# A two-layer attention and retention model on one core: the retention layer's token tiles placed ahead of the preceding output phase, and each next head's first value products placed at the end of the head before

## The chip, the cores and the metric

The kernel runs on one core of one Trainium2 chip. The metric is the device time of one execution in microseconds (us). The time before is 1820.17 us, the median of three runs (1818.12 to 1822.04). The core's engines are PE (TensorE: matmuls, with PEld for its weight loads), DVE (VectorE), ACT (ScalarE), POOL (GpSimd) and SP (SyncE, which here issues the loads).

## What is computed

Two layers over 512 latent tokens and 256 context tokens of width 1024, in float32. Layer 0 is windowed attention and an FFN, layer 1 bidirectional retention and an FFN. Each part is a normed input with a modulation, a mixer or FFN, and a gated addition to the stream. The part that matters here is the retention of layer 1, cut to its core:

```python
q_x, k_x, v_x, g_x = split(h_x @ w_qkvg)        # 4 heads: q, k 256 wide; v, g 512 wide
k_c, v_c = split(h_c @ w_qkvg[:, qk:2*qk + v])  # keys and values of the context
q_x = rope_2d(q_x, tables); k_x = rope_2d(k_x, tables) * k_scale
# per head, forward and backward scans, each from its final context state:
#   out = (q k^T * decay) v + q state * decay
mu, var = mean(o), variance(o)                  # over the 512 values of a head
y = (o - mu) * rsqrt(var + EPS) * gn_gain
out_x = (silu(g) * y) @ w_o
x = x + mx[2] * out_x
x = x + mx[5] * swiglu(modulate(rms_norm(x), mx[3], mx[4]), w_in, w_out)
```

## The kernel before

**Products in three matmuls.** Every float32 operand is split into two parts, hi (a copy on ACT, L164 or L139) and lo (a subtraction on DVE, L165 or L140), and a product is three matmuls: hi·hi, lo·hi, hi·lo. Weights come from HBM in pieces of 128x1024 float32 (512 KB) through SP's queue into one of two raw buffers (`wraw`) and are split into tiles `whi` and `wlo`, of which four pairs go round: two in the resident pool `rp` and two in the stage's own pool (`w_parts`).

**Seven products.** The FFNs of both layers and the retention's projections save an eighth of the matmuls: 2x2 blocks are multiplied by a scheme with seven products instead of eight, for which sums of token tiles (`token_sums`, L1120) and sums of weight pieces (L1268 to L1272, L1300 to L1306, L1362) are made on DVE first. "11", "12" and "22" name plain blocks, and the numbers 1 to 4 sums. `product_v` (L1171) makes value and gate products, two tiles of 128 tokens with 512 columns, 12 matmuls each; `product_q` (L1160) makes keys and queries.

**The stages around the change.** The last FFN output of layer 0 is `output(prev, True)` (L1075): for all latent and then all context tiles, matmuls (L147 to L149), a gated addition on DVE (L252), squares for the next norm on ACT (L208), their sum on DVE or POOL (L209), and the latent statistics once the latent tiles are through (L197 ends them). Then the pools of layer 0's FFN close, and those of the retention open: `hR` on the right side of the memory (token tiles `aq`, `hc`, sums `sA`), `qw`, `qa`, `qp` on the left. `latent_norm` (L1141) makes the token tiles: L1144 norms a tile into `qk`, L1147 (ACT) and L1148 (DVE) make hi and lo. `strips` (L1196) makes a head's decay factors. `context_norm` (L1153) does the context's norm.

**One head** (loop at L1223, four times): first value products "11" and "12" and the context's (`cv`), keys, then the query and key sum products (L1275 to L1289), rotation of queries and keys (`rope_pair`, L1183, DVE, POOL, ACT, DVE in a row), gate and value products (L1309 to L1317), scores and accumulation over six key tiles (L1322 to L1356), two more gate products (L1366, L1369), the norm of the output (L1380 to L1391), the gating (L1396), 16 transposes on PE (L1402), their copies (L1407, L1408) into eight `qk` tiles, and the output (`out_tile`, L1413), eight tiles of 12 matmuls. In the last head the output runs by halves of the tokens (L1440), with the statistics and the norm of the last FFN in it, and its first weights (`first_weights`, L1432). `first_two` (L1520) then makes the first two gate and up projections of that FFN; inside its first one `second_half` asks for the statistics of the second half of the tokens.

**What sets the order.** The kernel is written against tile pools. A planner orders each engine's instructions at build time: of those that its own model of the run holds to be ready, the one that was written first goes first. The order is then fixed, and each engine works it down. A tile that is laid over an older one waits for that one's last reader, tile by tile. A pool on the right side takes its room from the top down, and its tiles lie upward in the order in which their names are first asked for. `after(a, b)` puts an instruction behind others without a wait of its own. PSUM has eight banks: `pj` (2) and in the retention `X`, `Y`, `Z` (2 each).

The order of a head's end, which the change takes apart:

```python
        product_v(Zg, quarter_of(4), w22, False)     # L1369, last gate product
        ...                                          # norm of ov, gates: L1380 to L1396
        tps = [W4("Z"), W4("Z"), pj(), pj()]         # L1399
        for n in (2, 3, 0, 1):
            for e in range(4):
                nc.tensor.transpose(tps[e][:, n * P:(n + 1) * P], gate[n][:, e * P:(e + 1) * P], ident)
```

Of the kernel before, what the change touches and what calls it, by code (L numbers as in the profile page):

```python
# [16 lines left out]
KT = D // P  # L17
# [32 lines left out]
def dit_kernel(ctx, tc, xT, cT, crow, small, consts, masks, tabs0, tabs1, jtab, adaQ, adaN, adaT, wst, out):  # L50
# [104 lines left out]
    def project_pair(ws, hs, os, between=None):  # L155

        for k in range(KT):
            for w, o in zip(ws, os):
                ins = mm3(o, (w[0][:, k * P:(k + 1) * P], w[1][:, k * P:(k + 1) * P]), hs[k], k == 0, k == KT - 1)
            if k == 2 and between:  # L160
                between([ins])
# [687 lines left out]
    hq = F.enter_context(tc.tile_pool(name="hq", bufs=1, reuse_waits="tile", side="right"))  # L849
# [224 lines left out]
    assert not ada_q  # L1074
    output(prev, True)  # L1075
# [11 lines left out]
    H = ExitStack()  # L1087
    hpool[0] = H.enter_context(tc.tile_pool(name="hR", bufs=1, reuse_waits="tile", side="right"))
# [5 lines left out]
    h_sum = [(T(hpool[0], 512, "sA", 16, F32R), T(hpool[0], 512, "sA", 16, F32R)) for _ in range(KT)]  # L1094
# [14 lines left out]
    def t_qk(dt=F32R):  # L1109
        return T(qp, 512, "qk", 8, dt)  # L1110
# [9 lines left out]
    def token_sums(hm, part, sh2, sums):  # L1120

        q1, q2 = HALVES
        shift = mods[1, 0][:, part]
        nc.vector.tensor_tensor(sh2[:, 0:4], shift[:, 0:4], shift[:, 4:8], op=add)
        for k in range(4):
            t1, t2 = hm[k], hm[k + 4]
            nc.vector.scalar_tensor_tensor(t2[:, q2], t1[:, q2], sh2[:, k:k + 1], t2[:, q2], add, add)
# [25 lines left out]
    def context_norm(behind):  # L1153
        rms(1, bank=pj, behind=behind)
        h_ctx.extend(norm_mod(1, 1, 0, cres)[0])
# [15 lines left out]
    def product_v(os, a, w, first):  # L1171

        for t, o in enumerate(os):
            tok = slice(t * P, t * P + P)
            for k in range(4):
                whi, wlo = (p[:, k % 2 * 512:k % 2 * 512 + 512] for p in w[k // 2])
                xhi, xlo = (x[:, tok] for x in a(k))
                for i, (p, r) in enumerate(((xhi, whi), (xhi, wlo), (xlo, whi))):
                    ins = nc.tensor.matmul(o, p, r, start=first and k + i == 0, stop=k == 3 and i == 2,  # L1179
                                           skip_group_check=not first)  # L1180
        return ins
# [38 lines left out]

    hm = latent_norm()
    dx, dcx = strips(0)
    for hd in range(RH):  # L1223
# [4 lines left out]
        b11 = [split_chunk(chunk(bv + i)) for i in range(2)]  # L1228
        b21 = [split_chunk(chunk(bv + i)) for i in (2, 3)]
        Yv, Xv, cv = [W4("Z"), W4("Z")], [W4("X"), W4("X")], [pj(), pj()]  # L1230
        ins = product_v(Yv, quarter_of("11"), b11, True)
        if hd == 0:
            context_norm([ins])
        vt = [T(rp, 512, "res", 12) for _ in range(4)]
        for t in range(2):
            nc.scalar.copy(vt[t], Yv[t])
        product_v(Xv, quarter_of("12"), b21, True)
# [8 lines left out]
        if hd == 0:  # L1246
            token_sums(hm, 0, T(qp, 64, "sh2", 1), h_sum)
# [43 lines left out]
        kh = rope_pair(kt, cos1, sin1)  # L1291
# [58 lines left out]
        pend = None  # L1350
        for m in range(6):
            cur = scores(m)
            if pend is not None:
                accumulate(m - 1, *pend)
# [44 lines left out]
        tps = [W4("Z"), W4("Z"), pj(), pj()]  # L1399
# [4 lines left out]
        for e in range(4):  # L1404
# [4 lines left out]
            yt.append((hi, lo))  # L1409
        wpos[0] = chunk_base + 16 * hd + 12  # L1410
# [18 lines left out]
        hF = ctx.enter_context(tc.tile_pool(name="hF", bufs=1, reuse_waits="tile", side="right"))  # L1429
# [8 lines left out]
        hF_parts = lambda: (T(hF, 1024, "whi", 2, F32R), T(hF, 1024, "wlo", 2, F32R))  # L1438
        ln_exp_turn()
        for i, c in enumerate(HALVES):  # L1440
            for d in range(KT):
# [4 lines left out]
                if (i, d) in ((1, 3), (1, 5)):  # L1446
                    first_weights(hF_parts)
                if i == 1 and d == 1:
                    hm += [T(hF, 512, "hm", 8) for _ in range(KT)]
                    off_grid(hF, 48)  # L1450
                    hx += [(T(hF, 512, "hx", 16, F32R), T(hF, 512, "hx", 16, F32R)) for _ in range(KT)]
                    off_grid(hF, 16)
# [18 lines left out]
    ring += [rp, rp, hF, hF, fp, fp]  # L1471
# [34 lines left out]
    def seven():  # L1506
        g, u = w_raw(fp, 2), w_raw()
        b11 = w_parts(fp, 4)
        b22 = T(hF, 512, "hm", 8, F32R), T(hF, 512, "hm", 8, F32R)
# [209 lines left out]
```

## Time and profile before

| what | value |
|---|---|
| median of three runs | 1820.17 us (1818.12 to 1822.04) |
| profiled execution | 1813.7 us, span 1811.9 us, mean granted clock 0.99 |
| ACT, POOL busy | 836.5 us (46%), 161.6 us (9%) |
| last output phase of layer 0, PE | 871.65 to 906.5 us |
| retention, first product to last output matmul | 908.20 to about 1462 us |
| heads 1, 2, 3 begin on PE | 1058.12, 1192.14, 1324.86 us |
| granted clock at one half, in span time | 909.5 to 923.1, 977.7 to 984.5, 1032.3 to 1039.2, 1435.1 to 1438.5 us |

The span runs from the first to the last instruction of the profiled execution; the execution's own time is 1.8 us more. A row of the time views gives start, duration, engine, line, operation, output and inputs, shapes and count, and in brackets how long the engine had been idle and what ended that. A row of waits gives the instruction, what it waited for, total, times and longest. The granted clock is the share of full speed that the throttle gave PE.

### The profile page before, as it was taken

Reading aid. Unit: us, or ns where it says so; the run is one execution under the profiler, and the core shown is the slowest. Engines: PE = TensorE matmul, PEld = TensorE weight load, DVE = VectorE, ACT = ScalarE, POOL = GpSimd, SP = SyncE. Lnnn points to the kernel's source line nnn. Section 1 sums busy time; section 2 is a strip of 40 time slices with the busy share of each in tenths; the row PEclk is TensorE's granted clock in tenths of the full one; section 3 lists DMA queues with packets and bytes.
Section 4 is the critical chain, followed back from the end, with each engine's and each line's share of the span. In section 5 each row is a group of like instructions: output and inputs, shape, how many; then the busy total and the mean of one; then the engine's idle time right before and its main releaser. Section 6 shows DMA issues by size and latency. Waiting matters only on the chain.

```text
span 1811.9 us, 27643 instructions
## 1 busy us (share of the span) xinstructions
PE 1728.4 (95%) x10876; PEld 1531.3 (85%) x10876; DVE 1347.3 (74%) x2327; ACT 836.5 (46%) x1461; POOL 161.6 (9%) x291
## 2 busy tenths in 40 slices
PE   6999999999999999999979998999999999999999
PEld 4777776799999999999867787787787899999998
DVE  6697786786689877777698747847848898777774
ACT  5477676362424343333464524524524564445442
POOL 0035344000000000000001001001001010000000
PEclk9999999999999999999989999999999999999999
DMA  9510002542244444343233523524423333234232
GB/s 350 212 45 16 24 2 82 186 140 94 82 140 128 152 127 141 119 148 117 72 128 117 164 70 116 165 72 128 155 78 109 111 95 97 90 117 117 83 93 82
DMA packets 59891, 206.69 MB, mean 114 GB/s; under 512 B 6640, under 2 KB 7024, under 8 KB 59504
## 3 DMA queue, kind: packets, MB, share of 16 engines
q1 hardware_dynamic: 52848, 179.75, 30.8%
q0 software_dynamic: 6912, 25.17, 4.6%
q8 instruction: 85, 1.39, 0.3%
q14 instruction: 46, 0.38, 0.1%
HBM read 202.80 MB, written 2.10 MB: 113 GB/s over the span
## 4 chain that ended last, share of the span: by engine, by line
PE 71%; DVE 15%; DMA 5%; ACT 4%; issue 2%; POOL 2%; DVEq 0%; ACTq 0%; POOLq 0%; SPq 0%
PE Y L834 13%; PE Z L834 6%; PE pj L149 6%; PE pj L148 6%; PE pj L147 6%; PE Z L1179 4%; DMA wraw<-in_wst_dram 3%; DVE wlo L165 3%; PE X L834 3%; PE pT L706 2%; PE pO L718 2%; PE S L683 2%; PE pj L1179 2%; PE X L147 1%; PE Y L147 1%
## 5 line engine op out<-in xcount | busy, mean ns | idle before, releaser
L164 ACT CAST whi<-wraw 128x1024 fp32r<-128x1024 f32 x173 | 180.9, 1051 | 307.7 <-PE Z L149 73.1
L165 DVE TENSOR_TENSOR wlo<-wraw,whi 128x1024 fp32r<-128x1024 f32 x173 | 211.1, 1223 | 52.2 <-ACT whi L164 51.7
L834 PE MATMUL Y<-aq,whi 128*128 128x384 f32 x576 | 156.0, 335 | 0.5 <-ACT hn L973 0.5
L252 DVE SCALAR_TENSOR_TENSOR res<-pj,mod,res 128x512 f32<-128x512 f32 (+1 forms) x112 | 81.6, 729 | 64.7 <-PE pj L149 63.6
L139 ACT CAST whi<-wraw 128x1024 fp32r<-128x1024 f32 x84 | 87.9, 1048 | 85.1 <-PE Z L149 23.5
L140 DVE TENSOR_TENSOR wlo<-wraw,whi 128x1024 fp32r<-128x1024 f32 x84 | 102.9, 1226 | 28.1 <-ACT whi L139 27.3
L834 PEld LDWEIGHTS Y<-aq,whi 128*128 128x128 f32 x576 | 104.8, 188 | 1.2 <-ACT hn L973 0.8
L834 PE MATMUL Y<-aq,wlo 128*128 128x384 f32 x288 | 96.5, 335 | 1.6 <-DVE wlo L165 1.6
L101 ACT ACTIVATE pr<-pr,stat,qs 128x513 f32<-128x513 f32 (+2 forms) x96 | 74.3, 776 | 30.7 <-DVE stat L690 29.8
L1179 PE MATMUL Z<-whi,sA 128*128 128x512 f32 x256 | 81.9, 397 | 2.4 <-ACT gate L1311 2.2
L697 POOL TENSOR_SCALAR pr<-pr,stat 128x512 f32<-128x512 f32 (+2 forms) x96 | 67.1, 713 | 86.5 <-DVE stat L694 66.4
L270 DVE CUSTOM_DVE_ANT_0 y<-adaw,crow,small_sb 128x1024 bf16<-128x1024 f32 x48 | 61.4, 1280 | 13.8 <-DMA adaw<-in_adaT_dram 13.7
L147 PE MATMUL pj<-ax,whi 128*128 128x512 f32 x176 | 68.8, 391 | 1.1 <-DVE res L252 1.1
L1190 POOL TENSOR_TENSOR hn<-hn,sq 128x512 f32<-128x512 f32 x16 | 28.9, 1819 | 448.1 <-DVE sq L1189 432.0
L149 PE MATMUL pj<-ax,whi 128*128 128x512 f32 x176 | 68.6, 390 | 0.0
L148 PE MATMUL pj<-ax,wlo 128*128 128x512 f32 x176 | 68.5, 389 | 0.0
L706 PE MATMUL pT<-const_sb,pr 128*128 128x128 f32 x352 | 58.1, 284 | 9.9 <-POOL pr L697 7.6
L147 PE MATMUL pj<-act,whi 128*128 128x512 f32 x168 | 66.0, 393 | 0.0
L148 PE MATMUL pj<-act,wlo 128*128 128x512 f32 x168 | 65.9, 392 | 0.0
L149 PE MATMUL pj<-act,whi 128*128 128x512 f32 x168 | 65.5, 390 | 0.0
L706 PEld LDWEIGHTS pT<-const_sb,pr 128*128 128x128 f32 x352 | 38.8, 141 | 30.4 <-POOL pr L697 18.4
L684 DVE CUSTOM_DVE_ANT_0 pr<-S,mask,qs 128x256 f32<-128x256 f32 (+1 forms) x96 | 53.1, 567 | 14.3 <-PE S L683 7.9
(504 smaller groups left out, 5363.3 us busy)
## 6 DMA issues: line engine op xcount, KB each, us to landing
wraw<-in_wst_dram SPq DMA_DIRECT2D x238, 512.0 KB, 3.6
adaw<-in_adaT_dram POOLq DMA_DIRECT2D x32, 512.0 KB, 3.9
wx<-in_wst_dram SPq DMA_DIRECT2D x24, 512.0 KB, 4.5
adan<-in_adaQ_dram SPq DMA_DIRECT2D x16, 512.0 KB, 7.8
adan<-in_adaN_dram SPq DMA_DIRECT2D x16, 512.0 KB, 8.2
crow<-in_adaT_dram POOLq DMA_DIRECT2D x16, 512.0 KB, 4.2
res<-in_xT_dram SPq DMA_DIRECT2D x16, 256.0 KB, 5.4
adaw<-in_adaT_dram SPq DMA_DIRECT2D x8, 512.0 KB, 4.0
```

What stands on the lines that cost most here:

```text
L101: ins = nc.scalar.activation(*args, **kw)
L139: nc.scalar.copy(hi, raw)
L140: nc.vector.tensor_tensor(lo, raw, hi, op=sub)
L147: nc.tensor.matmul(o, whi, xhi, start=first, stop=False)
L148: nc.tensor.matmul(o, wlo, xhi, start=False, stop=False)
L149: return nc.tensor.matmul(o, whi, xlo, start=False, stop=last)
L164: nc.scalar.copy(hi, t)
L165: return nc.vector.tensor_tensor(lo, t, hi, op=sub)
L252: return nc.vector.scalar_tensor_tensor(res[d], o, mods[l, s][:, part, d:d + 1], res[d], mult, add)
L706: nc.tensor.transpose(tp[:, a * P:(a + 1) * P], self.pr[(0, 2, 1, 3)[a]][:, ki * P:(ki + 1) * P], ident)
L834: nc.tensor.matmul(o, p, r, start=first and k + i == 0, stop=k == 3 and i == 2, skip_group_check=not first)
L1179: ins = nc.tensor.matmul(o, p, r, start=first and k + i == 0, stop=k == 3 and i == 2, skip_group_check=not first)
```

## The change

No instruction is added or taken away; they are placed and ordered otherwise.

- **Token tiles ahead of the output.** The pool `hq` of layer 0's operand sums closes before `output(prev, True)`, and `hR` opens there; the sums `sA` get a pool of their own (`hS`) after it. The `qk` tiles (the normed tokens, later rotated queries and keys, at last the gated output) move from `qp` on the left into `hR`. The ring of weight tiles begins anew there.
- **Order in the first head.** The first value product stands right behind the latent norm; token sums are put behind the context norm; the first decay strips come behind the token sums.
- **Head ends.** The next head's first value product (`values_first`) stands between gates and transposes, its first context product (`context_values`) between transposes and output. The transposes write the `X` and `Y` banks, which held the head's outputs.
- **Inside a head.** Y2 is copied before Y; the keys' rotation stands behind the weights of gates and values; the last value product is cut in two, with the first scores between the halves.
- **Last FFN.** Its pool `hF` becomes three, `hM`, `hW`, `hX`, in this order from the top; the statistics of the second half are asked for after the sixth step of the first projection, not the third.

```diff
     assert not ada_q
+    Q.close()
+    H = ExitStack()
+    hpool[0] = H.enter_context(tc.tile_pool(name="hR", ..., side="right"))
+    wsel[0] = 0
     output(prev, True)
...
-    H = ExitStack()
-    hpool[0] = H.enter_context(tc.tile_pool(name="hR", ..., side="right"))
+    hS = H.enter_context(tc.tile_pool(name="hS", ..., side="right"))
...
     def t_qk(dt=F32R):
-        return T(qp, 512, "qk", 8, dt)
+        return T(hpool[0], 512, "qk", 8, dt)
...
-    def product_v(os, a, w, first):
-        for t, o in enumerate(os):
+    def product_v(os, a, w, first, tiles=(0, 1)):
+        for t in tiles:
+            o = os[t]
...
+    def values_first(hd):
+        w = [split_chunk(chunk(chunk_base + 16 * hd + 4 + i)) for i in range(2)]
+        Y = [W4("Z"), W4("Z")]
+        ins = product_v(Y, quarter_of("11"), w, True, (0,))
+        product_v(Y, quarter_of("11"), w, True, (1,))
+        return w, Y, ins
+
+    def context_values(w):
+        c = [pj(), pj()]
+        product_v(c, context_half(0), w, True)
+        return c
+
     hm = latent_norm()
-    dx, dcx = strips(0)
+    ahead_v = values_first(0)
     for hd in range(RH):
-        b11 = [split_chunk(chunk(bv + i)) for i in range(2)]
+        b11, Yv, ins = ahead_v
+        if hd == 0:
+            normed = context_norm([ins])
         b21 = [split_chunk(chunk(bv + i)) for i in (2, 3)]
-        Yv, Xv, cv = [W4("Z"), W4("Z")], [W4("X"), W4("X")], [pj(), pj()]
-        ins = product_v(Yv, quarter_of("11"), b11, True)
-        if hd == 0:
-            context_norm([ins])
...
-        product_v(cv, context_half(0), b11, True)
+        if hd == 0:
+            cv = context_values(b11)
         product_v(cv, context_half(1), b21, False)
...
         if hd == 0:
-            token_sums(hm, 0, T(qp, 64, "sh2", 1), h_sum)
+            token_sums(hm, 0, T(qp, 64, "sh2", 1), h_sum, [normed])
+            dx, dcx = strips(0)
...
         product_q(Y2, quarter_of(1), w1, True)
+        for e, o in halves(Y2):
+            nc.scalar.copy(qt[e][:, HALVES[1]], o)
         product_q(Y, quarter_of(3), w3, False)
         for e, o in halves(Y):
-            nc.scalar.copy(qt[e][:, HALVES[1]], o)
-        for e, o in halves(Y2):
             nc.vector.tensor_tensor(qt[e][:, HALVES[1]], qt[e][:, HALVES[1]], o, op=add)
...
         qh = rope_pair(qt, cos1, sin1)
-        kh = rope_pair(kt, cos1, sin1)
...
             w4.append(split_chunk(v21))
+        kh = rope_pair(kt, cos1, sin1)
...
-        product_v(Yv, quarter_of("22"), w4, False)
-        for t in range(2):
+        def last_values(t):
+            product_v(Yv, quarter_of("22"), w4, False, (t,))
             nc.scalar.copy(vt[2 + t], Yv[t])
+        last_values(0)
...
-        pend = None
-        for m in range(6):
+        pend = scores(0)
+        last_values(1)
+        for m in range(1, 6):
...
-        tps = [W4("Z"), W4("Z"), pj(), pj()]
+        if hd < RH - 1:
+            ahead_v = values_first(hd + 1)
+        tps = [W4("X"), W4("X"), W4("Y"), W4("Y")]
...
             yt.append((hi, lo))
+        if hd < RH - 1:
+            cv = context_values(ahead_v[0])
...
         H.close()
-        hF = ctx.enter_context(tc.tile_pool(name="hF", ..., side="right"))
+        hM, hW, hX = (ctx.enter_context(tc.tile_pool(name=n, ..., side="right"))
+                      for n in ("hM", "hW", "hX"))
...
-                project_pair(ahead[2 * f:2 * f + 2], half(i), (go[:, c], uo[:, c]), None if i + f else second_half)
+                project_pair(ahead[2 * f:2 * f + 2], half(i), (go[:, c], uo[:, c]), None if i + f else second_half, 5)
```

The tiles `hm` now come from `hM`, the weights `whi` and `wlo` of the last FFN from `hW`, and the normed tokens `hx` from `hX`.

More of the change, by code (lines that the diff above doesn't have):

```diff
@@ L159, in project_pair @@
                 ins = mm3(o, (w[0][:, k * P:(k + 1) * P], w[1][:, k * P:(k + 1) * P]), hs[k], k == 0, k == KT - 1)
-            if k == 2 and between:
+            if k == at and between:
                 between([ins])
@@ L1093, in dit_kernel @@
     W4 = lambda n: T(psR, 512, n, 2)
[L1094 removed]
+    h_sum = [(T(hS, 512, "sA", 16, F32R), T(hS, 512, "sA", 16, F32R)) for _ in range(KT)]
     h_first = [T(hpool[0], 512, "aq", 12, F32R) for _ in range(4)]
@@ L1118, in operands, with token_sums @@
         return of
-    def token_sums(hm, part, sh2, sums):
+    def token_sums(hm, part, sh2, sums, behind=()):
         q1, q2 = HALVES
@@ L1126, in token_sums @@
             t1, t2 = hm[k], hm[k + 4]
-            nc.vector.scalar_tensor_tensor(t2[:, q2], t1[:, q2], sh2[:, k:k + 1], t2[:, q2], add, add)
+            after(nc.vector.scalar_tensor_tensor(t2[:, q2], t1[:, q2], sh2[:, k:k + 1], t2[:, q2], add, add), behind)
             nc.vector.tensor_tensor(t1[:, q2], t1[:, q1], t1[:, q2], op=sub)
@@ L1154, in context_norm @@
         rms(1, bank=pj, behind=behind)
-        h_ctx.extend(norm_mod(1, 1, 0, cres)[0])
+        h, last = norm_mod(1, 1, 0, cres)
+        h_ctx.extend(h)
+        return last
     def context_half(i):
@@ L1437, in dit_kernel @@
         wx_parts = lambda: (T(qw, 1024, "wx", 4, F32R), T(qw, 1024, "wx", 4, F32R))
-        hF_parts = lambda: (T(hF, 1024, "whi", 2, F32R), T(hF, 1024, "wlo", 2, F32R))
+        hW_parts = lambda: (T(hW, 1024, "whi", 2, F32R), T(hW, 1024, "wlo", 2, F32R))
         ln_exp_turn()
```

28 lines of the change are left out of this document (15 added, 13 removed).

## The prediction

> **What bounds the kernel now.** I read the page first, then who waited for whom on PE from 906 to 1475 us (the retention layer and the entry to the last FFN), then the order of time of PE, DVE, ACT and SP around each long wait, then busy sums by stage.
>
> The page:
>
> ```profile
> span 1811.9 us, 27643 instructions
> PE 1728.4 (95%) x10876; PEld 1531.3 (85%) x10876; DVE 1347.3 (74%) x2327; ACT 836.5 (46%) x1461; POOL 161.6 (9%) x291
> PE 71%; DVE 15%; DMA 5%; ACT 4%; issue 2%; POOL 2%; DVEq 0%; ACTq 0%; POOLq 0%; SPq 0%
> ```
>
> PE is the bound: 71% of the chain that ended last, busy 95%. A change that adds and removes no instruction, as this one, can only win where PE stands still or runs at a lower granted clock. Waits of PE in the stretch that is touched (us in total, times, longest):
>
> ```profile
> PE Z L1179 <- DVE wlo L165: 16.2, 8, 10.2
> PE X L147 <- ACT qk L1407: 5.7, 4, 1.6
> PE pj L1333 <- DVE hn L1338: 4.1, 3, 1.4
> PE Z L1402 <- DVE gate L1396: 3.5, 4, 1.2
> PE Z L1179 <- ACT gate L1311: 2.2, 2, 1.9
> PE pj L1333 <- ACT qk L164: 2.1, 1, 2.1
> PE Y L1167 <- DVE gate L1283: 1.9, 3, 1.0
> ...
> PE pj L216 <- POOL y L209: 1.4, 1, 1.4
> ```
>
> Together 37 us, and every one is a wait that the change moves. The longest, 10.2, is the entry to the retention layer: the first value product waits for its weights' low half. In order of time DVE explains it (start, duration):
>
> ```profile
> 906.46 0.48 DVE L252 SCALAR_TENSOR_TENSOR res<-Z,mod,res 128x256 f32<-128x256 f32 x1 [0.95 <-PE Z L149]
> 906.86 1.41 DVE L1144 SCALAR_TENSOR_TENSOR qk<-res,acol,y 128x512 f32<-128x512 f32 x2
> ...
> 917.83 1.21 DVE L165 TENSOR_TENSOR wlo<-wraw,whi 128x1024 fp32r<-128x1024 f32 x1
> ...
> 919.36 1.21 DVE L165 TENSOR_TENSOR wlo<-wraw,whi 128x1024 fp32r<-128x1024 f32 x1
> ```
>
> The latent norm (L1144, L1148) begins only after the last context add, the splits of the value weights follow behind it, and PE stands from 908.9 to 919.1. The same view at the end of a head, on PE:
>
> ```profile
> 1031.81 0.44 PE L1402 MATMUL Z<-const_sb,gate 128*128 128x128 f32 x2 [1.19 <-DVE gate L1396]
> 1032.08 0.38 PE L1402 MATMUL pj<-const_sb,gate 128*128 128x128 f32 x2
> 1033.68 0.79 PE L147 MATMUL X<-qk,whi 128*128 128x512 f32 x1 [1.22 <-ACT qk L1407]
> ```
>
> Transposes wait for gates, the output for the transposes' copies. Busy sums by stretch (length; busy of PE, PEld, DVE, ACT, POOL; granted clock; DMA):
>
> ```profile
> 909.50:923.10 13.60, 4.01 (x10) 3.14 (x11) 13.60 (x25) 7.17 (x14) 0.00 (x0) 0.50 0.55 207
> 1032.30:1039.20 6.90, 5.68 (x15) 4.36 (x14) 5.09 (x6) 4.12 (x6) 0.00 (x0) 0.51 0.57 172
> 901.30:906.50 5.20, 5.12 (x41) 4.74 (x40) 1.98 (x6) 2.15 (x5) 2.56 (x4) 1.00 0.00 0
> ...
> 906.50:1017.50 111.00, 94.90 (x494) 80.74 (x495) 98.18 (x145) 59.96 (x99) 8.67 (x6) 0.91 0.40 127
> ```
>
> The granted clock halves around these waits, and a 512-column matmul then starts every 0.43 us, not 0.227. And DVE is busy 98.2 of 111 us in the first head: close behind PE.
>
> **The change, part by part.** A value product of two tiles is 24 matmuls, 5.45 us at 0.227.
>
> (a) Entry and first head, 906.5 to 1017.5. The token tiles now lie where the FFN's operand sums lay; their last reader, the last seven-product, ends at 871.7. So L1144 can start once the latent statistics are there (L197, done 901.4), five us earlier, in DVE's gaps: 5.20 less 1.98 busy, 3.2 us, some 2.7 of it usable, two to three of the four operand tiles needed first (1.07 each: 0.67 and 0.40 from start to start). With that pool moved, the value weights' split tiles also lie on room free since 871.7 or in the resident pool. Their data landed at 875.7 and 881.7, and DVE is busy only 11.7 of the 21.3 us before 901.3, so four low halves (1.22 each, 4.9 us) fit before the end of the output. Then PE has no reason to wait at 906.5: two value products and the context product, 96 matmuls, take 21.8 us instead of the 36.6 to 943.06. That is 14.8. Behind it the first head has waits of 1.9 and 2.1 and half clock from 977.7 to 984.5 (some 2.3 lost): at most 21 for PE. DVE gives less: 98.2 less 7.6 moved ahead leaves 90.6, so no more than 20.4; if it keeps all its 12.8 idle, only 7.6. The token sums (about 11 us) now queue behind the context norm (6.8), and the decay strips (1.65) behind them; all have to be through when PE comes to the first sum product at about 940, and I add them up to about 943, a new wait of 3 us where there was none. I take the middle, **14 us**, ends 7.6 and 20.4.
>
> (b) Inside heads 1 to 3. Copying Y2 before Y takes L1283 off the path of the next product: 1.9 us. Half of the last value product now stands between the first and second scores: 12 matmuls, 2.7 us, over waits on L1338 of 1.35; I take 1.0 of each. Moving the key rotation behind the weight splits brings those splits 4 us of DVE work earlier; they cost waits of 0.37 and 1.36, 0.35 and 1.35, and 1.83; I take half, 2.6. Against it the keys come late: multiply, POOL (1.6 to 2.0), ACT, DVE in a row, two such, 6 us after its start; 0.5 a head. 1.9 + 3.0 + 2.6 - 1.5 = **6 us**, ends 2 and 10.
>
> (c) Three head ends. The next head's first value product (5.45) now fills the time between gates and transposes, its context product (5.45) that between transposes and output. From 1028.4 PE needs 5.45 + 1.8 (16 transposes) + 5.45 + 21.8 (output) + 10.9 (second value and context halves) = 45.4, to 1073.8, against 1079.88: 6.1, of which 2.8 is half clock. At the other two, 48.5 against 45.4: 3.1 each, 12.2 in all. What must be in time: two weight low halves on DVE by 1028.4 and 1029.8. The output's first two stood there, ending 1027.7 and 1029.4, with the same split tiles and the same two raw buffers; the value weights take these places, and the output's move some 4 us on, needed first at 1041. On SP the two value loads go ahead of four output loads (3.6 us to landing), with 12 us of PE work over them. The Z banks are free from 1026.5 and 1030, before each is needed. I take **11.5**, ends -6.3 and 12.2.
>
> [...] The row: half clock from 1032.3 to 1039.2, though the longest wait just before was 1.22 us. [...]
>
> (d) End of the last head. Nothing fills it, and the transposes now write the banks that hold the outputs, so none starts before the last gate product (1433.2); before, half of them were done by 1431.8. That puts some 12 transposes, 1.2 us, on the path, and the half-clock stretch (1435.1 to 1438.5, 1.4 us lost) may lengthen: **-2 us**, ends 0 and -3.
>
> (e) Entry to the last FFN. The statistics of the second half are now asked for three steps later (6 matmuls of 0.12 each), which takes away the 1.36 wait on POOL. But by the order of requests in the pools (16 KB each counted from the top) the tiles for weights three and four now lie on the 16 KB of the rotated tiles, which the output reads to its end at about 1462; two splits (ACT 1.05, DVE 1.22 each) that stood at 1445 to 1452 come in front of the norm's last tiles. PE has 5.8 us of the first gate and up before it needs them. **+0.7**, ends -3 and 1.4.
>
> **Sum.** 14 + 6 + 11.5 - 2 + 0.7 = 30.2 us off the profiled execution's 1813.7 (span 1811.9): 1783.5. The median of the runs, 1820.17, lies 6.5 above that execution; taken from the median, **1790.0**. With the ends that (a) to (e) reach without a new mechanism, 9.6 (taking 6 for c) and 44, it is 1776 to 1811.
>
> **Rivals.**
> 1. DVE becomes the bound but nothing gets worse. For it: 98.2 of 111 us, hardly a gap from 906 to 950. Then (a) 8, (b) 2, (c) 8.5, (d) -3, (e) -1: 14.5, 1805.7. Chance 0.22.
> 2. All covers hold: (a) 20, (b) 9, (c) 12.2, (d) and (e) -1: 40, 1780. Chance 0.08.
> 3. The clock isn't won back at the head ends: (c) is 8.7, 1792.8. A stretch with short waits and 128-column transposes can still be granted half. Chance 0.08. [...]
> 4. Slower: DVE works its queue in order, and what the change puts further back comes last while PE's matmuls stand behind it. Place and price: the context norm ends where it did (939.6), then token sums, strips, key weights' sums and one split, 19 us, to 959 against 954.6: -4.5, and no gain in the rest of the head; value weights behind the last gate product (1031.8), first usable 1032.9, PE idle 4.5 and then 1.7 lost at half clock: 0, -3.1, -3.1; keys late by 2 in each of three heads: -6; (d) -3, (e) -3. Together -22.7: 1842.9. It decides once the splits for the next head stand behind the last L1396 and the sums behind 940. Against it: DVE is half idle before 906, and the order of instructions is planned by when they are ready. Chance 0.07.
> 5. It doesn't do what it says: the norm still starts after the last context add, and head ends win as much as (d), (e) and late keys lose: within 3.6 us of 1820. Chance 0.05.
>
> **Numbers.** Forecast 0.50, at 1780 to 1800; rivals 0.22, 0.08, 0.08, 0.07, 0.05. Faster by over 0.2% (3.6 us, about what a measurement of this kernel can tell from no change): 0.50 + 0.22 + 0.08 + 0.08 = 0.88; same 0.05; slower 0.07. The range leaves out rivals 4 and 5: 1776 to 1811.
>
> **What would show it.** L1144 starting near 901 to 903 and the first L1179 near 906.5 with no wait of 10 us and full clock (a); a new PE wait at the first product with the token sums (a, rival 1); no wait on L1283, and shorter ones on L1338 and on the splits (b), or a new one on the keys (rival 4); value products between the last gate product and the transposes with no wait before them (c); later transposes in the last head (d); no wait on POOL L209, and how late the splits for weights three and four stand (e). The forecast is wrong if DVE's order puts the next head's splits behind the gates, or if a stall of more than some 6 us opens before the sum products.

## The result, and the profile after

The changed kernel takes 1812.9 us (median of 9 runs, 1811.3 to 1816.3) where the kernel before takes 1819.8 (9 runs beside them, 1816.2 to 1822.4): a ratio of 0.9963, 95% interval 0.9952 to 0.9974. It is faster by 6.9 us, where 30.2 were forecast, and lies above the range of 1776 to 1811.

The profiled execution took 1812.0 us, span 1810.2. Its page, the lines that answer to those of before:

```profile
span 1810.2 us, 27644 instructions
PE 1732.1 (96%) x10876; PEld 1538.7 (85%) x10876; DVE 1352.0 (75%) x2327; ACT 835.0 (46%) x1461; POOL 163.9 (9%) x291
PE 69%; DVE 16%; DMA 6%; ACT 4%; issue 3%; POOL 2%; SPq 0%; DVEq 0%; ACTq 0%; POOLq 0%
```

PE is still the bound, with the same instructions. The page can't tell where the time went; the stretches between the same matmuls of both traces can (start to start, us):

| stretch (part of the prediction) | before | after | gain | forecast |
|---|---|---|---|---|
| start to last output matmul ahead of the layer | 906.1 | 908.0 | -1.8 | 0 |
| (a) to the first key product | 36.9 | 32.4 | 4.6 | |
| (a) to the first sum product | 11.5 | 12.4 | -0.9 | |
| (a) to the first head's gate product behind the scores | 62.9 | 67.2 | -4.2 | |
| (a) together | 111.4 | 111.9 | **-0.5** | 14 |
| (b) heads 1 to 3, first sum product to gate product | 187.6 | 186.7 | **0.9** | 6 |
| (c) three head ends, gate product to next key product | 180.6 | 168.5 | **12.1** | 11.5 |
| (d) last head, gate product to the first statistics matmul | 33.0 | 34.3 | **-1.4** | -2 |
| (e) from there to the last FFN's first output product on Z | 58.2 | 66.0 | **-7.8** | 0.7 |
| to the last matmul | 296.4 | 296.2 | 0.1 | 0 |

The pair of profiles shows 1.7 us. The first row is code that the change leaves alone: over the profiled executions here the last output phase begins anywhere from 871.6 to 877.0 us, so one pair can be some 5 us off. The rows below it gain 3.5 in all; why the medians differ by 6.9, this one pair of profiles does not show.

The waits of PE in the stretch that was touched (us in total, times, longest) name what took the place of the old ones:

```profile
PE Z L1187 <- ACT gate L1336: 8.6, 3, 2.9
PE Z L1187 <- ACT whi L164: 5.3, 2, 3.6
PE Z L1187 <- DVE wlo L165: 4.6, 2, 4.0
PE Z L1187 <- ACT gate L1333: 2.7, 3, 0.9
PE X L147 <- ACT hx L241: 2.6, 2, 1.4
```

The 1.8 and 10.2 us at the entry are now 1.8, 1.1 and 4.0. New are three waits of 2.9, one in each later head, on ACT's copy of a gate product (L1336). Before, the same copy was waited for twice, by 0.5:

```profile
PE Z L1179 <- ACT gate L1314: 1.0, 2, 0.5
```

**The entry.** DVE and ACT of the changed kernel in order of time (start, duration):

```profile
899.48 1.23 DVE L165 TENSOR_TENSOR wlo<-wraw,whi 128x1024 fp32r<-128x1024 f32 x1 [0.59 <-ACT whi L164]
...
903.42 1.24 DVE L1149 SCALAR_TENSOR_TENSOR qk<-res,acol,y 128x512 f32<-128x512 f32 x1
...
904.97 0.74 DVE L1149 SCALAR_TENSOR_TENSOR qk<-res,acol,y 128x512 f32<-128x512 f32 x1
...
915.89 1.21 DVE L165 TENSOR_TENSOR wlo<-wraw,whi 128x1024 fp32r<-128x1024 f32 x1
917.03 0.74 DVE L1153 SCALAR_TENSOR_TENSOR aq<-qk,mod,aq 128x512 fp32r<-128x512 f32 x1
```

```profile
908.63 0.42 ACT L208 ACTIVATE sq<-res 128x256 f32<-128x256 f32 x1 [0.82 <-DVE res L252]
908.95 1.03 ACT L164 CAST whi<-wraw 128x1024 fp32r<-128x1024 f32 x1
```

The norm does start early, at 903.4. But of the first two value weights only one is split early, at 898.4 on ACT and 899.5 on DVE; its tile is in the resident pool. The other lies in the layer's own pool `qp`. By the layout of the pools its room had last been read at about 873, but the closed pool that held this room also held the activations that the output reads to its end. ACT splits it only at 908.95, 1.0 us behind the last output matmul, and its low half stands on DVE at 915.89 behind nearly the whole norm.

**The middle of the first head** (first sum product to gate product) was to lose its waits and its half clock; it became 4.2 us longer. Busy sums before and after (columns as in the prediction):

```profile
954.60:1017.50 62.90, 58.66 (x302) 49.57 (x301) 51.57 (x64) 31.05 (x49) 7.01 (x4) 0.95 0.43 132
```

```profile
952.70:1019.90 67.20, 60.92 (x301) 51.08 (x302) 56.35 (x69) 32.66 (x51) 6.94 (x4) 0.92 0.40 125
```

PE's waits there sum to 6.8 us (4.2 before), the longest 3.6 for a high half from ACT. The clock is at one half from 954.9 to 958.4 and from 975.4 to 982.2; before, only from 977.7 to 984.5. DVE is busy 4.8 us more in this stretch: work that stood ahead of the first sum product now stands behind it.

**Heads 1 to 3.** ACT and PE of the second head:

```profile
1116.79 0.62 ACT L164 CAST qk<-hn 128x512 fp32r<-128x512 f32 x1 [4.79 <-POOL hn L1198]
1117.32 0.58 ACT L1336 COPY gate<-Z 128x512 f32<-128x512 f32 x1
```

```profile
1114.68 0.39 PE L1187 MATMUL Z<-whi,sA 128*128 128x512 f32 x1
1117.95 0.50 PE L1187 MATMUL Z<-whi,aq 128*128 128x512 f32 x1 [2.88 <-ACT gate L1336]
```

```profile
1111.00:1117.90 6.90, 3.16 (x13) 2.17 (x12) 5.09 (x7) 2.10 (x4) 3.92 (x2) 1.00 0.60 205
1118.70:1122.10 3.40, 3.40 (x9) 2.60 (x9) 2.29 (x3) 1.47 (x2) 0.00 (x0) 0.51 0.24 45
```

The gate product is done at about 1115, but on ACT a copy of the rotated keys, which waits 4.8 us for POOL and starts at 1116.8, stands in front of the gate copy, which starts at 1117.3. PE's bank comes free 2.9 us late, and then the granted clock is 0.51 for 3.4 us (busy sums by stretch, as in the prediction).

**The entry to the last FFN.** DVE:

```profile
1446.82 0.42 DVE L197 SCALAR_TENSOR_TENSOR y<-sq,y 128x256 f32<-128x256 f32 x1
1447.41 0.48 DVE L1450 SCALAR_TENSOR_TENSOR res<-Y,mod,res 128x256 f32<-128x256 f32 x1 [0.16 <-PE Y L149]
...
1451.73 0.48 DVE L1450 SCALAR_TENSOR_TENSOR res<-X,mod,res 128x256 f32<-128x256 f32 x1 [0.96 <-PE X L149]
1452.13 1.74 DVE L238 SCALAR_TENSOR_TENSOR hm<-res,acol,y 128x256 f32<-128x256 f32 x3
```

The statistics are ready at 1447.2. DVE idles 0.96 us ahead of each of three output adds, and still the norm (L238) comes only at 1452.1, 4.9 us later, when PE is at the last output matmul (1452.9). It then goes ahead even of the last output add, which follows at 1458.8. Before, the norm came right behind the statistics, with output adds among its steps:

```profile
1456.26 0.48 DVE L197 SCALAR_TENSOR_TENSOR y<-sq,y 128x256 f32<-128x256 f32 x1
1456.77 1.36 DVE L238 SCALAR_TENSOR_TENSOR hm<-res,acol,y 128x256 f32<-128x256 f32 x2
1458.06 0.47 DVE L1421 SCALAR_TENSOR_TENSOR res<-X,mod,res 128x256 f32<-128x256 f32 x1
```

By the layout of the pools, the tiles that the norm writes lie on the context's normed tiles (`hc`), which the last head's context products read last: their room was free.

**Theory.** T1: the order of each engine is written when the program is built; there, an instruction on a tile of a pool that is opened over a closed one stands behind the last reader of that whole pool, though the tile's own room may have been read for the last time long before (here at about 873, by the layout of the pools). It holds the first value weight at the entry, and at the FFN the norm, whose room lay in one pool with the rotated tiles. (The two weight splits there lie on the rotated tiles themselves.) T2: the loss in heads 1 to 3 is ACT's order, keys ahead of gates. T3: with these gone DVE bounds the first head (rival 1 of the prediction). Rivals: the order in which the program asks, the later request for the second statistics, or the amount of DVE work alone.

### The profile page after: what moved, and what is told of

Read it like the earlier page. It is cut to its first block, busy times and chain, and to the rows that moved or that the text cites. A ratio compares the mean times of both kernels' runs of the same rounds, so it can differ in the third digit from the quotient of the medians.

```text
span 1810.2 us, 27644 instructions
## 1 busy us (share of the span) xinstructions
PE 1732.1 (96%) x10876; PEld 1538.7 (85%) x10876; DVE 1352.0 (75%) x2327; ACT 835.0 (46%) x1461; POOL 163.9 (9%) x291
## 4 chain that ended last, share of the span: by engine, by line
PE 69%; DVE 16%; DMA 6%; ACT 4%; issue 3%; POOL 2%; SPq 0%; DVEq 0%; ACTq 0%; POOLq 0%
PE Y L834 12%; PE Z L834 6%; PE pj L148 6%; PE pj L149 6%; PE pj L147 6%; PE Z L1187 5%; PE X L834 3%; DVE wlo L165 3%; DMA wraw<-in_wst_dram 3%; PE pT L706 2%; DVE y L270 2%; DMA adaw<-in_adaT_dram 2%; PE pO L718 2%; PE S L683 2%; PE pj L1187 2%
## 5 line engine op out<-in xcount | busy, mean ns | idle before, releaser
L270 DVE CUSTOM_DVE_ANT_0 y<-adaw,crow,small_sb 128x1024 bf16<-128x1024 f32 x48 | 61.4, 1278 | 14.5 <-DMA adaw<-in_adaT_dram 14.4
L1198 POOL TENSOR_TENSOR hn<-hn,sq 128x512 f32<-128x512 f32 x16 | 30.1, 1886 | 436.2 <-DVE sq L1197 432.6
L1187 PEld LDWEIGHTS Z<-whi,sA 128*128 128x128 f32 x256 | 49.1, 192 | 19.6 <-ACT gate L1333 5.6
```

The source lines that it names most:

```text
L270: after(nc.vector.tensor_tensor_reduce(junk, w, cr[:, s * 1024:(s + 1) * 1024], 1.0, sm_t[:, C_ADAB + l * 48 + j:C_ADAB + l * 48 + j + 1], ...
```

## The experiments

Each was timed in 3 rounds beside the kernel before unless noted; ratios are to it, lengths by the stretches above.

**1. Both first value weights in the resident pool** (T1 at the entry).

```diff
+    wsel[0] = 4
     hm = latent_norm()
```

> The changed kernel with one line more: the ring of weight tiles is set on by one ahead of the first value product, so that both of its weight pieces are split into the resident pool and none into the pool that opens after the output. Theory (a tile of a pool that takes the room of a closed pool is planned only when that whole pool is through, though the room itself is free): both splits stand ahead of the latent norm, the 4.0 us wait on the low half and its half clock go; from the last output matmul to the first key product 25 to 28 us (32.1 in the changed kernel, 36.6 before, 21.8 of matmuls), the execution 4 to 7 us shorter. Rival (DVE works the splits behind the norm because they were written behind it): no change, 32.

1808.4 us, 0.9926 (0.9899 to 0.9953). Both low halves are now through before the norm:

```profile
903.14 1.23 DVE L165 TENSOR_TENSOR wlo<-wraw,whi 128x1024 fp32r<-128x1024 f32 x1 [0.60 <-ACT whi L164]
...
906.96 1.22 DVE L165 TENSOR_TENSOR wlo<-wraw,whi 128x1024 fp32r<-128x1024 f32 x1
...
908.49 0.84 DVE L1149 SCALAR_TENSOR_TENSOR qk<-res,acol,y 128x512 f32<-128x512 f32 x1
```

The last output matmul to the first key product takes 25.6 us (32.4 changed): T1's number. But from there to the first sum product it takes 14.0 instead of 12.4, with new waits, and the middle of the head is no shorter (67.9). PE's waits from 906 to 1000 us:

```profile
PE Z L1187 <- ACT whi L164: 2.9, 1, 2.9
PE Y L1174 <- ACT whi L164: 2.4, 1, 2.4
PE Y L1174 <- DVE wlo L165: 1.7, 1, 1.7
```

So the edit itself gives 4.4 us, in the first head (111.9 to 107.5). The profiled execution also gained 3.2 in heads 1 to 3 (186.7 to 183.5), where the edit was not aimed: the same three waits of 2.9 are there, but in two of the three heads the clock stayed at 1.00 behind them. That part is luck as far as these runs show:

```profile
1116.70 0.50 PE L1187 MATMUL Z<-whi,aq 128*128 128x512 f32 x1 [2.88 <-ACT gate L1337]
```

```profile
1117.20:1121.60 4.40, 4.40 (x21) 3.60 (x20) 3.14 (x5) 2.22 (x4) 0.00 (x0) 1.00 0.31 72
```

**2. The same splits asked for ahead of the norm, same tiles.**

```diff
+    w0 = [split_chunk(chunk(chunk_base + 4 + i)) for i in range(2)]
     hm = latent_norm()
-    ahead_v = values_first(0)
+    ahead_v = values_first(0, w0)
```

> The changed kernel with the two splits of the first value product written ahead of the latent norm, in the same tiles as before. Theory (held by the closing pools): the first piece, which lies in the late pool, is still split at the end of the output only; at most 1 to 2 us of the wait go, from the last output matmul to the first key product 30 to 32 us. Rival (order of writing): 25 to 28, as good as the other.

1808.2 us, 0.9927 (0.9900 to 0.9954); entry 27.2 us: the rival's number. Both count. The high half on ACT still comes just after the last output matmul (0.7 us after it, 1.0 in the changed kernel), so the pool does hold it; but its low half on DVE comes 2.1 us after that matmul (910.5) and not 7.9, in the middle of the norm:

```profile
912.62 1.21 DVE L165 TENSOR_TENSOR wlo<-wraw,whi 128x1024 fp32r<-128x1024 f32 x1
```

The pool sets the earliest place, the order of asking the place among what is ready then. My theory had left the second out.

**3. The rotated tiles in a pool of their own** (T1 at the last FFN).

```diff
+    hQ = H.enter_context(tc.tile_pool(name="hQ", bufs=1, reuse_waits="tile", side="right"))
-        return T(hpool[0], 512, "qk", 8, dt)
+        return T(hQ, 512, "qk", 8, dt)
-                      for n in ("hM", "hW", "hX"))
+                      for n in ("hW", "hM", "hX"))
```

> The changed kernel with the rotated and gated tiles (qk) in a right-side pool of their own above hR, and at the end the three pools in the order hW, hM, hX, so that only hW lies over a pool that the output still reads. Theory (whole pools are waited for): the norm of the last FFN begins within 1 us of its statistics (4.9 us after them in the changed kernel), the waits on L241 and L242 and most of the half clock from 1456.6 to 1463.4 go, 5 to 8 us less. Rival (the two late weight splits stand in front of the norm's tiles on ACT and DVE): these splits stay late, so at most 1.5 us less.

1810.0 us, 0.9926 (0.9900 to 0.9952). The norm comes right behind the statistics (1447.4 and 1447.9), as expected. Its tiles still lie on `hc`, as in the changed kernel; only the rotated tiles are in another pool. But last transpose to first output product on Z is 84.3 us (86.4 changed, 77.8 before): 2.0 won, neither number. The weight pool was now the one over the rotated tiles, and its two splits stayed 31 us behind the last transpose (13.5 in the head ends alone). They hold the raw buffers, the next loads go out later, ACT then waits 4.4 and 2.7 us for raw weights, and PE 4.2 behind them:

```profile
1488.86 0.62 ACT L164 CAST hm<-wraw 128x512 fp32r<-128x512 f32 x1 [4.40 <-DMA wraw<-in_wst_dram]
...
1492.68 0.62 ACT L164 CAST hm<-wraw 128x512 fp32r<-128x512 f32 x1 [2.70 <-DMA wraw<-in_wst_dram]
```

```profile
PE pj L147 <- DVE res L252: 4.2, 1, 4.2
```

**4. The activation tiles over the rotated tiles.** The last FFN's activations are written only after the layer; with their pool laid over the rotated tiles, norm and weights lie on room that is through.

```diff
-        hW, hM, hX = (ctx.enter_context(tc.tile_pool(name=n, bufs=1, reuse_waits="tile", side="right"))
-                      for n in ("hW", "hM", "hX"))
+        fa, hM, hW, hX = (ctx.enter_context(tc.tile_pool(name=n, bufs=1, reuse_waits="tile", side="right"))
+                          for n in ("fa", "hM", "hW", "hX"))
...
-    fa = F.enter_context(tc.tile_pool(name="fa", bufs=1, reuse_waits="tile"))
```

> The changed kernel with the rotated tiles in a right pool of their own at the top (as in the run with an own pool), and at the end of the layer the last FFN's activation tiles, which are written only after it, laid over that pool first; its norm and weight pools then lie on room that is through with the sums. Theory (a pool opened over one that is still read is put behind the last reader as a whole): the two weight splits stand some 13 to 16 us behind the last transpose as in the head ends alone (31 with the own pool), the norm tiles within 1 us of the statistics, the loads go on time; last transpose to first output product on Z 77.5 to 79.5 us (86.4 changed, 84.3 own pool, 77.8 before), 7 to 9 us less than the changed kernel, 0.991 to 0.993. Rival (the later request of the second half's statistics or the amount of DVE work costs the 8 us): 84 to 86, 0.996.

1806.5 us, 0.9909 (0.9873 to 0.9944). Last transpose to Z: 77.6 us, all of the 8.8 back. DVE:

```profile
1443.49 1.22 DVE L165 TENSOR_TENSOR wlo<-wraw,whi 128x1024 fp32r<-128x1024 f32 x1
...
1449.91 0.42 DVE L197 SCALAR_TENSOR_TENSOR y<-sq,y 128x256 f32<-128x256 f32 x1
1450.37 0.85 DVE L238 SCALAR_TENSOR_TENSOR hm<-res,acol,y 128x256 f32<-128x256 f32 x1
```

The split stands between output adds, the norm right behind the statistics. Only which tiles lie where, and in which pool, was changed: with experiment 3, T1 is shown here.

**5. The second statistics asked for early, as before.**

```diff
-                project_pair(ahead[2 * f:2 * f + 2], half(i), (go[:, c], uo[:, c]), None if i + f else second_half, 5)
+                project_pair(ahead[2 * f:2 * f + 2], half(i), (go[:, c], uo[:, c]), None if i + f else second_half)
```

> The changed kernel with the statistics of the last FFN's second half asked for where the kernel before asks (behind the third of eight steps and not the sixth). Theory (the pools' order costs the 8 us at this entry, not the place of the request): the request comes 2.2 us earlier on PE and the wait of 1 to 2 us on POOL returns, last transpose to first output product on Z 85.5 to 87.5 us (86.4 changed), 0.996 to 0.997. Rival (the later request pushes the second half's norm and all behind it): 78 to 80, 0.992.

1815.1 us, 0.9959 (0.9939 to 0.9979); last transpose to Z 86.8, and the wait on POOL returns:

```profile
PE pj L216 <- POOL y L209: 1.6, 1, 1.6
```

The rival falls. The later request saves that wait and costs nothing that shows.

**6. The key rotation back behind the query rotation.**

```diff
         qh = rope_pair(qt, cos1, sin1)
+        kh = rope_pair(kt, cos1, sin1)
...
-        kh = rope_pair(kt, cos1, sin1)
```

> The changed kernel with the key rotation back behind the query rotation, ahead of the weight splits; all else as changed. Stretch read: heads 1 to 3, first sum product to first gate product behind the scores; 62.0, 63.0 and 61.6 us in the changed kernel, 63.4, 62.1 and 62.1 before. Theory (the rotation's copies stand on ACT ahead of the gate copies, so PE waits 2.9 us for the gate and then runs 3.4 us at half clock): the waits on the gate copy fall below 0.6, the half clock behind them goes, the waits on the low halves of the splits come back with 1.4 to 2.0; 59 to 60.5 a head, 6 to 9 us less than the changed kernel, a ratio of 0.991 to 0.993 to the kernel before. Rival (the keys' place in the queue is not what makes the gate late, DVE's amount of work is): the waits of 2.9 stay or move to the splits in full, 61.5 to 63 a head, 0.996.

**7. The key rotation behind the second pair of gate copies**, its own ACT copies ordered after them.

```diff
-        kh = rope_pair(kt, cos1, sin1)
...
-        for t in range(2):
-            nc.scalar.copy(gate[2 + t], Yv[t])
+        copies = [nc.scalar.copy(gate[2 + t], Yv[t]) for t in range(2)]
+        kh = rope_pair(kt, cos1, sin1, copies)
```

> The changed kernel with the key rotation put behind the second pair of gate copies, and its ACT copies made to follow them. Same stretch as for the keys put back. Theory: the gate copies come as soon as the product is there, waits on them below 0.6 us and no half clock behind, the splits stay early; 58 to 59.5 a head, 8 to 12 us less than the changed kernel, 0.989 to 0.992. Rival (the keys are the bound: what the gate gains the first scores lose): the wait moves to the first scores with 2.5 us or more and the half clock with it, 61 to 63 a head, 0.995 to 0.997.

Put back (6): 1809.8 us, 0.9926 (0.9899 to 0.9954); heads 1 to 3 182.3 us (186.7 changed). Behind the copies (7): 1808.2 us, 0.9913 (0.9886 to 0.9940); 179.7. PE's waits from 1085 to 1420 us, first (6), then (7):

```profile
PE Z L1187 <- DVE wlo L165: 9.0, 4, 2.7
```

```profile
PE pj L1360 <- DVE qk L1201: 3.7, 3, 1.3
```

The waits of 2.9 on the gate go in both. In (6) the splits are late instead, by 2.7 a head: the wait moved almost whole, as the rival said, and in two of the three heads the clock is at one half for 3.4 us there (from 1110.5 and from 1240.2). The heads (60.6, 61.1 and 60.7) lie between the two expectations, so (6) alone does not decide. In (7) the first scores wait 1.1 to 1.3 for the keys, and the granted clock stays at 1.00 through these heads; they are up to 0.9 us longer than expected. T2 is shown by (7).

**8. The head ends alone**, on the kernel before: the next head's value and context products moved, the transposes on the output banks, nothing else.

```diff
+        if hd < RH - 1:
+            ahead_v = values_first(hd + 1)
-        tps = [W4("Z"), W4("Z"), pj(), pj()]
+        tps = [W4("X"), W4("X"), W4("Y"), W4("Y")]
...
+        if hd < RH - 1:
+            cv = context_values(ahead_v[0])
```

> The kernel before with the head ends of the change alone: the next head's first value product between gates and transposes, its first context product between transposes and output, transposes into X and Y. Theory (head ends win by themselves what the changed kernel shows there, 6.2 + 3.2 + 3.2, and lose 1 at the last head): 11 us less than before, ratio 0.994. Rival (they need the rest of the change, for instance the ring's new place): 6 us or less.

1808.2 us, 0.9930 (0.9908 to 0.9952), head ends 6.2, 3.2 and 3.2 us shorter. By the medians, this part by itself is worth more than the whole change: its entry stays (37.3 us), its FFN entry too (77.8).

**9. A lighter first head** (T3; read from its profile alone), on the kernel of 1.

```diff
-            nc.vector.tensor_tensor(t1[:, q2], t1[:, q1], t1[:, q2], op=sub)
...
-            nc.vector.scalar_tensor_tensor(t2[:, q1], t2[:, q1], shift[:, k + 4:k + 5], t1[:, q1], add, sub)
```

> The kernel with both first pieces in the resident pool, with two of the four DVE instructions for each pair of token tiles left out of the token sums of the first head (and of the last FFN, which shares the function): eight less, 0.4 to 0.5 us each, so the sums hold other values. Theory (with the entry's wait gone DVE is the bound from the end of the output to the first sum product, busy 39.7 of 39.6 us): last output matmul to first sum product 36 to 36.6 us instead of 39.6, and the waits of 2.4 and 1.7 us at the first sum product fall to 1 or less together. Rival (ACT's queue or the weights' transfer sets when the first sum product's weights are ready): 39 to 40 and the waits stay.

Last output matmul to first sum product: 37.1 us, not 39.6; the wait of 2.4 at the first sum product is gone, and that of 1.7 is 0.7. It isn't the 36.0 to 36.6 expected: the entry still takes 25.6, and the key products behind it 11.5, as in the later heads, without a wait, so that is PE's own time. Busy sums over that stretch in experiment 1 and in this one (length; PE, PEld, DVE):

```profile
911.50:951.10 39.60, 35.48 (x197) 29.66 (x195) 39.22 (x74) 26.52 (x48) 1.87 (x2) 1.00 0.39 131
```

```profile
907.90:945.10 37.20, 35.38 (x198) 29.78 (x196) 36.98 (x66) 25.34 (x45) 1.88 (x2) 1.00 0.43 139
```

With the entry's wait gone, DVE has hardly any idle time left (39.2 of 39.6). That alone would not show it to be the bound, since it is as full here (37.0 of 37.2); that the waits go when it has less to do, does. T3 holds up to the first sum product. Over the whole first head, 107.5 us became 103.9: 3.6 less, about what eight instructions of 0.42 to 0.48 us take.

**10. Edits 1, 4 and 7 together** (5 rounds).

> The changed kernel with three edits that each alone took time off it: both first value weights' pieces in the resident pool, the key rotation behind the second pair of gate copies, and the activation tiles over the rotated tiles at the end. If the three theories name separate causes the gains add, each in its own stretch: last output matmul to first sum product 39.5 us (44.7 changed), heads 1 to 3 from first sum product to gate product 179 to 181 in all (186.7 changed), last transpose to first output product on Z 77.5 to 78.5 (86.4): some 19 us off the changed kernel, 1793 to 1796, a ratio of 0.984 to 0.987 to the kernel before. Rival (they overlap: what one frees, the others were already waiting behind): 0.989 to 0.991, as the best of the three alone.

1793.2 us, 0.9857 (0.9838 to 0.9876), faster than both kernels. Output to first sum product 39.6, heads 1 to 3 179.1, last transpose to Z 76.4: the gains add, so the causes are separate.

**11. On top of that, the queries' rotation behind the weight splits in the first head** (5 rounds).

```diff
-        qh = rope_pair(qt, cos1, sin1)
+        if hd:
+            qh = rope_pair(qt, cos1, sin1)
...
             w4.append(split_chunk(v21))
+        if not hd:
+            qh = rope_pair(qt, cos1, sin1)
```

> The kernel with all three edits, and in the first head alone the query rotation put behind the weight splits for the second to fourth value and gate products. Stretch read: first sum product to first gate product of the first head, 68.2 us with the three edits (59.2 to 60.0 in the later heads), with a wait of 2.8 us for a high half that ACT copies behind a copy of the rotated queries, and half clock around it. Theory (that high half is late because DVE forms its weight sum, 970.6, behind the rotation's multiplies and ACT copies it behind the rotated queries): the wait falls below 0.6 us, the half clock with it, 63.5 to 65.5 us, 3 to 5 us less in all, 0.982 to 0.984 of the kernel before. Rival (the queries are then what comes last: the first scores wait 2.5 us or more for them, or the weights' transfers set the splits): 67 to 70, 0.985 to 0.988.

1790.6 us, 0.9840 (0.9812 to 0.9868), but the stretch is 68.3 us, as before the edit (68.2); the profiled execution's 2.9 us less were already there at the last output matmul (907.4 against 910.4). The wait on the high half went, and came back doubled on a gate copy, not at the scores:

```profile
PE Z L1188 <- ACT gate L1338: 5.9, 1, 5.9
```

```profile
976.24 0.62 ACT L1201 CAST qk<-hn 128x512 fp32r<-128x512 f32 x1 [3.62 <-POOL hn L1199]
976.77 1.06 ACT L1338 COPY gate<-Z 128x512 f32<-128x512 f32 x2
```

It is T2's pattern again. My reading of this stretch, that one late high half costs it 3 to 5 us, falls. What would shorten the first head's middle stays open.

## Why the prediction was wrong

**Sign right, size wrong**: two terms of five carried most of the error. Of the 30.2 forecast, (a) took 14.5, (e) 8.5 and (b) 5.1; (c) and (d) each came out 0.6 better.

(a) The step that failed first is "their data landed at 875.7 and 881.7, and DVE is busy only 11.7 of the 21.3 us before 901.3, so four low halves (1.22 each, 4.9 us) fit". It argued from room, data and a free engine. An instruction needs a fourth thing: its place in the engine's order. One of the two weights that the first product needs was held by its pool until the last output matmul, then queued behind the norm (experiments 1 and 2). The norm's early start was right, but little came of it: against the last output matmul it started 5.3 us earlier than before and ended 1.4 earlier.

This step is less than half of what (a) missed: mended, it returns 4.4 of the 14.5 (experiment 1), and the first head then gives 3.9 us (111.4 to 107.5), not 14. The second step that failed is "98.2 less 7.6 moved ahead leaves 90.6": DVE's work between the last output matmul and the gate product fell only from 98.2 to 95.8 us, and 4.8 us of it moved into the head's middle, which lost 4.2 us where its waits and half clock (6.3 in the prediction's figures) were to go. That DVE's load is what makes the high half late there is not shown; experiment 11 moved the wait and didn't shorten the stretch. The "new wait of 3 us" at the first sum product measured 1.6 with the entry still late and 4.0 once it was mended, and DVE as the next bound, rival 1, is what experiments 1 and 9 show up to there. The end of 7.6 that I took for the case "if it keeps all its 12.8 idle" was no lower end, since it counted neither the 7.6 as uncertain nor more half clock.

(b) The three waits named did go or shrink: none on DVE's hn at the first scores (4.1 us before), none on low halves in these heads, 1.4 on the sum product's gate (1.9). What failed is "the keys come late: 0.5 a head". The chain of multiply, POOL, ACT, DVE was the right one, but it was priced for who waits for the keys; the price is paid by what stands behind them on ACT, the gate copy: 2.9 us and then, in this profile, half clock from 1118.7 to 1122.1. Rival 4 asked just this of the work that is put further back (what stands behind it); the sum for (b) didn't ask it of ACT.

(c) Right, term by term: 6.2, 3.0 and 3.0 against 6.1, 3.1 and 3.1. The value product follows the gate product without a gap, transposes and context product too. PE, and busy sums by stretch:

```profile
1035.96 0.39 PE L1187 MATMUL Z<-whi,aq 128*128 128x512 f32 x1
1036.19 0.38 PE L1429 MATMUL X<-const_sb,gate 128*128 128x128 f32 x2
...
1037.85 0.48 PE L1187 MATMUL pj<-whi,hc 128*128 128x512 f32 x1
```

```profile
1034.10:1041.00 6.90, 6.90 (x40) 5.93 (x40) 4.56 (x7) 5.65 (x9) 0.00 (x0) 1.00 0.55 167
```

The granted clock is 1.00 where it was 0.51. Rival 3 falls: the waits of 1.2 us are gone, and the clock came back. What the prediction didn't look at: before, the other two head ends had waits as long (1.1 and 1.5, 1.1 and 1.4 us) at a clock of 1.00. So the 2.8 us of half clock are those of one head end in one profiled execution.

(d) -1.4 against -2: right.

(e) The place was right ("the tiles for weights three and four now lie on the 16 KB of the rotated tiles"), the price wrong: -7.8 against ends of -3 and 1.4. The step that failed is that two splits "come in front of the norm's last tiles". In fact the whole norm was held until the last output matmul, because its room lay in one pool with the rotated tiles, which are read to the end (experiments 3 and 4). In this stretch PE then waits 5.1 us instead of 2.8, and runs 6.8 at half clock (1456.6 to 1463.4) where there was none. So this is a failed mechanism, not a mis-sized term.

The upper end of the range, 1811, was made of ends "without a new mechanism"; two parts, (a) and (e), had the same new one in common, and the first head's middle, whose cause stays open, took as much of (a) again.

## What to carry to other kernels

Ahead of "it has room, data and an idle engine, so it comes early", ask what orders the instruction: which pool its tile is opened over and who reads that pool last, and what stands before it in its engine's order. When a chain with a slow link (here POOL, a median of 1.6 us for an add of 128x512, L1198, and 2.8 at most) is moved, price what is queued behind its waiting steps on each engine that it crosses. And where an order is planned from pools, lay what is written latest over what is read longest; that alone gave back 8.8 us here.

## What the runs showed of the hardware

In each of heads 1 to 3 of the changed kernel, a wait of 0.9 us and, some 6 us later, one of 2.9 were followed by 3.4 us at a granted clock of 0.50 to 0.51 (from 1118.7, 1248.5 and 1378.2). The same pair of waits in experiment 1 was followed by it in the last of the three heads alone; in the first of them the clock was 1.00 from 1117.2 to 1121.6. Waits of 0.9 and, some 8 us later, 1.1 to 1.3 us left the clock at 1.00 (experiment 7). Before the change, waits of 0.5, 1.2 and 1.2 us (at 1030.1, 1031.8 and 1033.7) went with a clock of 0.51 from 1032.3 to 1039.2, while 1.1 and 1.5 us at the next head end left it at 1.00:

```profile
1168.10:1175.00 6.90, 5.40 (x25) 4.36 (x26) 6.16 (x7) 4.60 (x7) 0.00 (x0) 1.00 0.63 168
```

So these runs give no length of a single wait from which the clock falls.

Of the eight DVE multiplies of 128x512 at L1149 in the changed kernel, five took 0.74 us (as at 904.97), two 1.24 and 1.23 (903.42 and 906.03) and one 0.82 (909.64). As these three began, POOL was in an add of 0.73 to 0.74 us (from 903.37, 905.97 and 909.19). One of the five also ran beside an add (POOL from 910.44), and there the add took 1.27. Before the change all eight (L1144) took 0.74 to 0.75, also beside POOL's add at 907.60, which took 1.27:

```profile
903.37 0.73 POOL L209 TENSOR_TENSOR y<-y,sq 128x256 f32<-128x256 f32 x1 [0.58 <-ACT sq L208]
```
